# The SSD scan of a hybrid decoder step in three steps per chunk, its elementwise tiles on VectorE, and the scan's mix loaded as whole tiles

## The chip, the cores and the metric

The kernel runs on 1 core of one Trainium2 chip. The metric is the device time of one launch in microseconds; three launches of the kernel before are shown. TensorE is called PE below, its weight loads PEld, VectorE DVE, ScalarE ACT, GpSimd POOL, and SP is the engine from whose queue the transfers here are issued.

## The reference, cut to what matters

One step of a one-layer decoder: a prompt of 1024 tokens and 8 samples of 8 new tokens each (64 rows) go through one input projection, two parallel mixers, one output projection, a squared-ReLU MLP and a final norm, all in float32. The mixers are an HGRN2 recurrence of 8 heads and a Mamba-2 SSD scan of 16 heads in 2 groups of 8. The change is in the second.

```python
log_a = (dt * a)...; xdt = xs * dt[..., None]
cum = jnp.cumsum(log_a, axis=2)                       # per chunk of 128 tokens
seg = cum[:, :, :, None] - cum[:, :, None, :]
decay = jnp.exp(jnp.where(causal, seg, -jnp.inf))
cb = jnp.einsum('cbtgn,cbsgn->cbtsg', cm, bm)
y_intra = jnp.einsum('cbtsg,cbtsgr,cbsgrp->cbtgrp', cb, decay, xdt)
...
def step(s, inp):                                     # over the chunks, in order
    y = jnp.einsum('btgn,bgrpn->btgrp', c_c, s) * fs_c[..., None]
    s = cd_c[..., None, None] * s + jnp.einsum('bsgn,bsgr,bsgrp->bgrpn', b_c, te_c, xdt_c)
    return s, y
...
y = y + d_skip[:, None] * xs
y = rmsnorm(y * silu(z), m_norm)                      # per group of 512 columns
mix = concatenate([o_hg, y]);  x = x + mix @ w_out
```

The samples run the same step with their own state per sequence (`state_ssm`), with 8 tokens as one chunk.

## The kernel before, in words

The kernel goes through its stages in this order: norm and the first chunk of the value projection (`stage01`, with `dt_math`, which leaves `cum`, `te`, `fs` and `cd` in SBUF and the transposed `cum` in DRAM as `cumd`), the SSD stage (`ssd`), the HGRN2 heads (`hgrn`), the output projection (`outproj`), and the MLP (`up_phase`, `down_phase`). Most products are made of three float32r products of high and low parts (`mm3`); the small ones of the scan are plain float32, which the trace shows as two records for each.

The SSD stage in program order: six tiles of the convolution for group 0 (`conv_tile`, whose results go to DRAM as `xtd`, `bcd`, `btd`), the gate columns `z_chunk` 0 and 1 (to DRAM as `szd`), the eight chunks of group 0 in two halves (`ssd_half`), the sample rows of group 0 (`ssd_sample`), `z_chunk` 2 and 3, the six other convolution tiles, the sample rows of group 1, the eight chunks of group 1, and `v_chunk` 1 to 3, the rest of the value projection.

A planner orders the instructions of each engine before launch: it takes the program order as the priority, lets later work through where an earlier instruction is not ready by its assumed durations, and thereby puts matmuls of `z_chunk`, `conv_tile`, `v_chunk` and of the first HGRN2 head between those of the scan. At run time each engine goes through its own list in that order and waits where an operand is late. Transfers are issued from the queue of SP, in order as well.

One chunk of the scan before, by line: three loads (`em` L645, the broadcast rows of `cumd`, 128x1024; `sz` L647; `x` L649); on POOL the subtraction of `cum` from `em` (L650), on DVE the minimum with 0 (L651), on ACT one exponential of 128x1024 (L652), on DVE the product with the masked B-C product `cbm` (L653); in `ssd_x` `xdt` on DVE (L695), `te` on POOL (L696) and the skip term on DVE (L697); the matmuls `pyi` (L658), `pdd` (L660) and eight of `py` (L671); the new state from POOL (L663) and DVE (L666); the output from DVE (L672, L674) and POOL (L676); then `ssd_out`: the gate on POOL (L704), the square on ACT (L706), `rstd` in six small steps on DVE and ACT (L162 to L168), the scale on ACT (L708), four transposes `pyt` (L711) and the product with `m_norm` on DVE (L713), stored to `mixd`.

In `ssd_sample`, for each of four pairs of heads and each half of the eight sequences, the state is transposed and split, two matmuls of 512 columns (L766, L767) apply it to all rows, and `own_sequence` (L244) copies each row's own part out of the four with four predicated copies on DVE.

The last HGRN2 head is followed by `mix_half` (L831): sixteen loads of half tiles (128x544) of the scan's part of the mix, eight for the first half of the tokens (t = 0) and eight for the second, each split into a high part on ACT (L202) and a low part on DVE (L203). The first product of `outproj` needs all eight of t = 0. The raw tiles take slots of the ring `wk` (10 slots of 128x1088), which the head's own work tiles use too; the split parts lie where the normalised input lay, which is read last by the head's gate product.

Of the kernel before, what the change touches and what calls it, by code (L numbers as in the profile page):

```python
# [15 lines left out]
P = 128  # L16
# [3 lines left out]
NB = 8  # L20
# [37 lines left out]
class Kernel:  # L58
# [146 lines left out]
    def mm3(self, ps, sh, sl, mh, ml, start, stop):  # L205
        nc = self.nc
        nc.tensor.matmul(ps, sh, mh, start=start, stop=False)  # L207
        nc.tensor.matmul(ps, sh, ml, start=False, stop=False)  # L208
        return nc.tensor.matmul(ps, sl, mh, start=False, stop=stop)  # L209
# [15 lines left out]
    def per_sequence(self, pool, hi, lo, name, tag=None):  # L225

        gp = self.nc.gpsimd
        oh = pool.tile([P, NB, P], F32R, name=self.nm(name + "h"), tag=tag or name + "h", bufs=4 if tag else 1)
# [115 lines left out]
    def tm_gemm(self, wt, i, tot, pool):  # L344
# [10 lines left out]
        if i == NC:  # L355
            t = pool.tile([P, 260], F32, name=self.nm("st"), tag="st", bufs=3)[0:NS, :tot]
# [5 lines left out]
    def v_chunk(self, pool, j, s0=None, dtb=None, wt=None):  # L362
# [7 lines left out]
        for i in range(NT):  # L370
# [4 lines left out]
            ps = self.tm_gemm(wt, i, 260, pool)  # L375
            rows = P if i < NC else NS
            st = pool.tile([P, 260], F32, name=self.nm("st"), tag="st", bufs=3)
# [6 lines left out]
    def z_chunk(self, pool, j):  # L384
# [3 lines left out]
        for i in range(NT):  # L388
            ps = self.tm_gemm(wt, i, 256, pool)
            rows = P if i < NC else NS  # L390
            R = slice(0, rows)
            st = pool.tile([P, 260], F32, name=self.nm("sz"), tag="st", bufs=3)
# [3 lines left out]
            nc.sync.dma_start(self.szd[i * P:i * P + rows, 256 * j:256 * (j + 1)], st[R, 0:256])  # L396

    def stage01(self):
        nc, a, cst = self.nc, self.a, self.cst
        with self.tc.tile_pool(name="s0", bufs=2) as s0:  # L400
# [20 lines left out]
            self.v_chunk(s0, 0, s0, dtb, wt)  # L421
# [103 lines left out]
    def ssd(self):  # L525
        nc, a = self.nc, self.a
        with ExitStack() as es:
# [3 lines left out]
            self.cs = g.tile([P, 12, 27], F32, name="cs", bufs=1)  # L531
            for f in (10, 8, 0, 1, 2, 3):
                self.conv_tile(f)
            self.z_chunk(g, 0)
            self.z_chunk(g, 1)
            st = self.ssd_half(0, 0, None)
            st = self.ssd_half(0, 1, st)
            self.ssd_sample(0)
            self.z_chunk(g, 2)
            self.z_chunk(g, 3)  # L540
            self.ssd_final(0, st)
# [11 lines left out]
            self.ssd_sample(1)  # L553
            st = self.ssd_half(1, 0, None)
            st = self.ssd_half(1, 1, st)
            self.ssd_final(1, st)
            self.v_chunk(g, 1)
            self.v_chunk(g, 2)
            self.v_chunk(g, 3)

    C2 = {"sz": 3, "x": 3, "xdt": 3, "te": 2, "st": 3, "ms": 2}
# [4 lines left out]
    def em(self, name, shape):  # L566
        return self.g.tile(shape, F32, name=self.nm(name), tag="em", bufs=4)
# [60 lines left out]
    def ssd_half(self, gi, hf, st):  # L628
        nc, a, g, ps = self.nc, self.a, self.g, self.ps
        h0 = gi * 8  # L630
        sl = slice(hf * 512, (hf + 1) * 512)
        bt, ct, btok, cbm = (g.tile([P, 4, P], F32, name=self.nm(t), tag=t, bufs=b)
                             for t, b in (("bt", 1), ("ct", 2), ("btok", 2), ("cbm", 1)))
        nc.sync.dma_start(bt, self.bcd[gi][:, sl].rearrange("p (c t) -> p c t", c=4))
        nc.sync.dma_start(ct, self.bcd[2 + gi][:, sl].rearrange("p (c t) -> p c t", c=4))
        nc.sync.dma_start(btok, self.btd[gi][sl, :].rearrange("(c p) n -> p c n", p=P))
        pc = ps.tile([P, 4, P], F32, name=self.nm("pcb"), tag="sm", bufs=3)
        for j in range(4):
            nc.tensor.matmul(pc[:, j, :], bt[:, j, :], ct[:, j, :], start=True, stop=True)
        nc.vector.tensor_tensor(out=cbm, in0=pc, in1=bc(self.tri, 1, 4), op=ALU.mult)  # L640
        for j in range(4):
            c = 4 * hf + j
            rows = slice(c * P, (c + 1) * P)
            em = self.em("em", [P, 8, P])
            nc.sync.dma_start(em, self.cumd[c * MH + h0:c * MH + h0 + 8, :].partition_broadcast(P))  # L645
            sz = self.c2("sz", [P, 512])
            nc.sync.dma_start(sz, self.szd[rows, gi * 512:(gi + 1) * 512])  # L647
            x = self.c2("x", [P, 8, HD])
            nc.sync.dma_start(x.rearrange("p h d -> p (h d)"), self.xtd[rows, gi * 512:(gi + 1) * 512])  # L649
            nc.gpsimd.tensor_tensor(out=em, in0=em, in1=bc(self.cum[:, c, h0:h0 + 8], 2, P), op=ALU.subtract)  # L650
            nc.vector.tensor_scalar(out=em, in0=em, scalar1=0.0, scalar2=None, op0=ALU.min)  # L651
            nc.scalar.activation(em, em, AF.Exp)  # L652
            nc.vector.tensor_tensor(out=em, in0=em, in1=bc(cbm[:, j, :], 1, 8), op=ALU.mult)  # L653
            xdt, te = self.ssd_x(x, P, c, h0)
            pi = None
            if c > 0:
                pi = ps.tile([P, 512], F32, name=self.nm("pyi"), tag="sm", bufs=3)
                nc.tensor.matmul(pi, ct[:, j, :], st, start=True, stop=True)  # L658
            pd = ps.tile([P, 512], F32, name=self.nm("pdd"), tag="sm", bufs=3)
            nc.tensor.matmul(pd, btok[:, j, :], te.rearrange("p h d -> p (h d)"), start=True, stop=True)  # L660
            stn = self.c2("st", [P, 512])
            if c > 0:
                nc.gpsimd.tensor_tensor(out=stn.rearrange("p (h d) -> p h d", d=HD),  # L663
                                        in0=st.rearrange("p (h d) -> p h d", d=HD),
                                        in1=bc(self.cd[:, c, h0:h0 + 8], 2, HD), op=ALU.mult)
                nc.vector.tensor_tensor(out=stn, in0=pd, in1=stn, op=ALU.add)  # L666
            else:
                nc.vector.tensor_copy(stn, pd)
            py = ps.tile([P, 8, HD], F32, name=self.nm("py"), tag="sm", bufs=3)
            for h in range(8):  # L670
                nc.tensor.matmul(py[:, h, :], em[:, h, :], xdt[:, h, :], start=True, stop=True)  # L671
            nc.vector.tensor_tensor(out=x, in0=py, in1=x, op=ALU.add)  # L672
            if c > 0:
                nc.vector.tensor_tensor(out=xdt, in0=pi.rearrange("p (h d) -> p h d", d=HD),  # L674
                                        in1=bc(self.fs[:, c, h0:h0 + 8], 2, HD), op=ALU.mult)
                nc.gpsimd.tensor_tensor(out=x, in0=x, in1=xdt, op=ALU.add)  # L676
            st = stn
            self.ssd_out(gi, x.rearrange("p h d -> p (h d)"), sz, P, c * P)
        return st
# [887 lines left out]
```

## Time and profile before

| what | value |
|---|---|
| median of 3 runs | 1862.22 us (1861.55 to 1867.1) |
| profiled execution, its own time | 1862.58 us |
| its span, first to last instruction | 1860.9 us |
| PE busy | 1804.0 us, 97% of the span |
| DVE busy | 1346.1 us, 72% |
| ACT busy | 866.9 us, 47% |
| POOL busy | 558.1 us, 30% |
| PE's granted clock, mean | 0.991 of full speed |

The span leaves out 1.7 us of the profiled execution's own time. PE is busy almost throughout, so the places to look at are the few stretches in which it is not, and those in which its clock is below 1.00.

### The profile page before, as it was taken

The page shows a single profiled execution, that of the slowest core. Times are in us where ns is not written, and L with a number is a line of the kernel's source. Part 1 is how long each engine was busy: PE and PEld are TensorE (multiplying, and loading weights), DVE is VectorE, ACT ScalarE, POOL GpSimd, SP SyncE. Part 2 cuts the span into 40 slices and gives each one's busy share as a digit, 9 for nine tenths or more (in the row PEclk, how much of TensorE's full clock was granted, in tenths as well). Part 3 has the DMA queues.
Part 4 walks back from the last instruction along what each step waited for, and adds up shares of the span by engine and source line. Part 5 has one row for each costly group of instructions (what it writes and reads, how often), then busy time and mean ns, then how long its engine had stood idle before and what let it go on. Part 6 is the DMA issues. An engine that isn't in the chain of part 4 may idle for free.

```text
span 1860.9 us, 35593 instructions
## 1 busy us (share of the span) xinstructions
PE 1804.0 (97%) x13352; PEld 1734.6 (93%) x13352; DVE 1346.1 (72%) x2599; ACT 866.9 (47%) x1897; POOL 558.1 (30%) x606
## 2 busy tenths in 40 slices
PE   7999999998999999999899999999999999999998
PEld 7999889997899999999799998999999989999998
DVE  7677888858867766666864477987888767777863
ACT  8575445733254444444532464545554453323322
POOL 5413552226642223323300122222233223222320
PEclk9999999999999999999999999999999999999999
DMA  8444455455442222222276762555555675755621
GB/s 265 123 127 137 133 145 148 121 168 167 124 115 72 63 82 61 82 84 73 78 237 200 226 182 78 190 179 197 199 202 196 208 267 192 267 178 193 210 90 71
DMA packets 329495, 285.47 MB, mean 153 GB/s; under 512 B 26197, under 2 KB 268481, under 8 KB 329322
## 3 DMA queue, kind: packets, MB, share of 16 engines
q1 hardware_dynamic: 329322, 283.19, 48.7%
q8 instruction: 105, 1.72, 0.4%
q14 instruction: 68, 0.56, 0.1%
HBM read 184.61 MB, written 98.24 MB: 152 GB/s over the span
## 4 chain that ended last, share of the span: by engine, by line
PE 77%; DVE 9%; DMA 6%; ACT 3%; issue 2%; POOL 2%; SPq 1%; DVEq 0%; POOLq 0%; ACTq 0%
PE sx L1299 15%; PE mm L209 11%; PE mm L208 11%; PE mm L207 11%; PE sy L1299 7%; PE sz L1299 4%; DVE wl L203 2%; PE mk L207 1%; PE mk L209 1%; PE mk L208 1%; DMA wr<-in_w_down_dram 1%; PE pf L207 1%; PE pf L208 1%; PE pf L209 1%; DMA em<-cumd 1%
## 5 line engine op out<-in xcount | busy, mean ns | idle before, releaser
L202 ACT CAST wh<-wr 128x512 fp32r<-128x512 f32 (+3 forms) x354 | 203.1, 582 | 256.1 <-PE mm L208 98.6
L203 DVE TENSOR_TENSOR wl<-wr,wh 128x512 fp32r<-128x512 f32 (+3 forms) x354 | 237.2, 675 | 93.8 <-ACT wh L202 88.3
L209 PE MATMUL mm<-hh,wl 128*128 128x384 f32 (+1 forms) x840 | 279.7, 333 | 0.0
L207 PE MATMUL mm<-hh,wh 128*128 128x384 f32 (+1 forms) x840 | 277.6, 330 | 1.9 <-ACT raw L584 1.9
L208 PE MATMUL mm<-hl,wh 128*128 128x384 f32 (+1 forms) x840 | 279.0, 332 | 0.0
L1299 PE MATMUL sx<-th,wh 128*128 128x272 f32 x1248 | 243.0, 290 | 5.8 <-ACT u L1350 2.9
L1299 PEld LDWEIGHTS sx<-th,wh 128*128 128x128 f32 x1248 | 195.9, 189 | 10.0 <-ACT u L1350 5.3
L1299 PE MATMUL sx<-th,wl 128*128 128x272 f32 x624 | 179.3, 288 | 0.0
L1256 POOL TENSOR_TENSOR ws<-wr 128x384 f32<-128x384 f32 (+2 forms) x35 | 40.8, 1165 | 427.2 <-DMA wr<-in_w_down_dram 195.2
L209 PEld LDWEIGHTS mm<-hh,wl 128*128 128x128 f32 x840 | 158.1, 188 | 4.6 <-issue 3.7
L207 PEld LDWEIGHTS mm<-hh,wh 128*128 128x128 f32 x840 | 158.4, 189 | 3.5 <-ACT raw L584 2.6
L208 PEld LDWEIGHTS mm<-hl,wh 128*128 128x128 f32 x840 | 158.3, 188 | 1.4 <-issue 0.5
L208 PE MATMUL mm<-wl,hh 128*128 128x260 f32 (+1 forms) x512 | 152.4, 298 | 0.0
L207 PE MATMUL mm<-wh,hh 128*128 128x260 f32 (+1 forms) x512 | 151.6, 297 | 0.6 <-ACT hh L307 0.6
L209 PE MATMUL mm<-wh,hl 128*128 128x260 f32 (+1 forms) x512 | 150.1, 294 | 0.0
L1299 PE MATMUL sy<-th,wh 128*128 128x272 f32 x736 | 142.7, 290 | 2.4 <-ACT wh L202 2.3
L1299 PE MATMUL sx<-td,wh 128*128 128x272 f32 x672 | 131.5, 289 | 1.4 <-ACT acc L1442 1.1
L1299 PEld LDWEIGHTS sy<-th,wh 128*128 128x128 f32 x736 | 116.7, 190 | 3.2 <-ACT wh L202 2.7
L1299 PEld LDWEIGHTS sx<-th,wl 128*128 128x128 f32 x624 | 117.6, 189 | 0.2 <-DVE wl L203 0.2
L207 PE MATMUL mm<-mh,wh 128*128 128x272 f32 x384 | 110.0, 290 | 6.6 <-ACT mh L202 4.7
L208 PE MATMUL mm<-ml,wh 128*128 128x272 f32 x384 | 110.6, 289 | 0.0
L209 PE MATMUL mm<-mh,wl 128*128 128x272 f32 x384 | 110.1, 288 | 0.0
(510 smaller groups left out, 4937.8 us busy)
## 6 DMA issues: line engine op xcount, KB each, us to landing
td<-th SPq DMA_DIRECT2D x112, 272.0 KB, 3.0
td<-td SPq DMA_DIRECT2D x112, 272.0 KB, 5.5
wr<-in_w_in_dram SPq DMA_DIRECT2D x44, 512.0 KB, 4.3
wr<-in_w_out_dram SPq DMA_DIRECT2D x32, 512.0 KB, 4.5
wr<-in_w_up_dram SPq DMA_DIRECT2D x32, 512.0 KB, 4.2
u2d<-u SPq DMA_DIRECT2D x50, 272.0 KB, 2.2
ur<-u2d SPq DMA_DIRECT2D x50, 272.0 KB, 5.1
wr<-in_w_down_dram SPq DMA_DIRECT2D x64, 192.0 KB, 2.9
```

Source lines behind the costliest of these rows:

```text
L202: nc.scalar.copy(hi, x)
L203: (engine or nc.vector).tensor_tensor(out=lo, in0=x, in1=hi.bitcast(F32), op=ALU.subtract)
L207: nc.tensor.matmul(ps, sh, mh, start=start, stop=False)
L208: nc.tensor.matmul(ps, sh, ml, start=False, stop=False)
L209: return nc.tensor.matmul(ps, sl, mh, start=False, stop=stop)
L1256: (engine or self.nc.gpsimd).tensor_tensor(out=out_, in0=x, in1=y, op=op)
L1299: nc.tensor.matmul(acc, w_[:, k, :], b_[:, cols], start=first and k == 0 and q == 0, stop=k == nk - 1 and q == 2, skip_group_check=True)
```

## The change

- The scan of a group is one function, `ssd_group`, in three steps per chunk: `ssd_pre` (loads), `ssd_mid` (`ssd_x` and the decay), `ssd_prod` (the matmuls, state and output sum), and after them `ssd_end` (`ssd_out`). In program order the loads of chunk c+1 come ahead of the products of chunk c, then the decay of chunk c+1, then the end of chunk c-1.
- No large tile of the chunk is worked on by POOL: `te`, the decayed state, the sum of both output parts and the gate product go to DVE. The decay no longer subtracts: DVE takes the minimum of `em` and the broadcast `cum` (tensor-tensor instead of tensor-scalar), and ACT makes eight exponentials of 128x128, one per head, each with the negated `cum` (`ncum`) as its bias.
- The `em` loads of group 0 get an ordering edge behind the last matmul of the first six convolution tiles (`mark`).
- `ssd_sample`: eight masked copies of `cts` are laid into a zeroed tile `cm` on POOL, and sixteen matmuls of 128 columns per pair of heads add up each row's own part in PSUM; the predicated copies are gone, and ACT copies the result out. The sample rows of group 0 come after all eight chunks.
- Buffers: `em` 5 instead of 4, `xdt` 2 instead of 3; the staging tiles of `z_chunk` and `v_chunk` come from the ring `res` (4) instead of `st` (3).
- The scan's mix is loaded as eight whole tiles (128x1088). Four loads, with the splits of t = 0, come in program order ahead of the sample rows of the last head, four behind them; the splits of t = 1 follow from the same tiles.

The diff, cut to its core:

```diff
+            self.mark = self.last_mm
...
+    def ssd_group(self, gi):
+        if gi:
+            self.ssd_sample(gi)
+        self.ssd_pre(gi, 0)
+        self.ssd_mid(gi, 0)
+        for c in range(NC):
+            if c + 1 < NC:
+                self.ssd_pre(gi, c + 1)
+            st = self.ssd_prod(gi, c, st)
+            if c + 1 < NC:
+                self.ssd_mid(gi, c + 1)
+            if c:
+                self.ssd_end(gi, c - 1)
+        self.ssd_final(gi, st)
+        self.ssd_end(gi, NC - 1)
+        if gi == 0:
+            self.ssd_sample(gi)
...
+        ld = nc.sync.dma_start(em, self.cumd[c * MH + h0:c * MH + h0 + 8, :].partition_broadcast(P))
+        if gi == 0:
+            self.after(ld, self.mark)
...
+    def decay(self, em, cbm, rows, c, h0):
+        nc.vector.tensor_tensor(out=em, in0=em, in1=bc(self.cum[0:rows, c, h0:h0 + 8], 2, em.shape[2]), op=ALU.min)
+        for h in range(8):
+            nc.scalar.activation(em[:, h, :], em[:, h, :], AF.Exp, bias=self.ncum[0:rows, c, h0 + h:h0 + h + 1])
+        nc.vector.tensor_tensor(out=em, in0=em, in1=bc(cbm, 1, 8), op=ALU.mult)
...
-                nc.gpsimd.tensor_tensor(out=stn.rearrange("p (h d) -> p h d", d=HD),
+            nc.vector.tensor_tensor(out=stn.rearrange("p (h d) -> p h d", d=HD),
...
-        nc.gpsimd.tensor_tensor(out=te[r], in0=xdt[r], in1=bc(self.te[r, c, h0:h0 + 8], 2, HD), op=ALU.mult)
+        nc.vector.tensor_tensor(out=te[r], in0=xdt[r], in1=bc(self.te[r, c, h0:h0 + 8], 2, HD), op=ALU.mult)
...
-        nc.gpsimd.tensor_tensor(out=y[r_], in0=y[r_], in1=sz[r_], op=ALU.mult)
+        nc.vector.tensor_tensor(out=y[r_], in0=y[r_], in1=sz[r_], op=ALU.mult)
...
+        cm = g.tile([P, NB, 2, NB, TS], F32R, name=self.nm("cm"), tag="em", bufs=5)
+        nc.gpsimd.memset(cm.bitcast(F32), 0.0)
+        for b in range(NB):
+            nc.gpsimd.tensor_copy(cm[:, b, :, b, :], cts.bitcast(F32).rearrange("p (a b t) -> p a b t", a=2, t=TS)[:, :, b, :])
...
-                nc.tensor.matmul(pi, cts, sth, start=True, stop=False)
-                nc.tensor.matmul(pi, cts, stl, start=False, stop=True)
-                self.own_sequence(yf[:, j, :], pi, 4 * hf)
+                for q in range(4):
+                    b = 4 * hf + q
+                    for i, st_ in enumerate((sth, stl)):
+                        nc.tensor.matmul(pi, cm[:, b].rearrange("p a s t -> p (a s t)"), st_[:, q, :],
+                                         start=b == 0 and i == 0, stop=b == NB - 1 and i == 1)
+            nc.scalar.copy(yf[:, j, :], pi)
...
+    def mix_ssd(self, ks):
+        for k in ks:
+            m = self.g.tile([P, T], F32, name=self.nm("mraw"), tag="wk", bufs=10)
+            self.nc.sync.dma_start(m, self.mixd[KO + k])
+            self.mraw.append(m)
+            self.mix[1, 0].append(self.mix_part(m[:, 0:TH]))
+    def mix_other(self):
+        self.mix[1, 1] = [self.mix_part(m[:, TH:]) for m in self.mraw]
...
+        if h == NH - 1:
+            self.hs.close()
...
+            self.mix_ssd(range(4))
```

## Rows read from the trace of the kernel before

**Rows 1.** The page, part 1: busy time, share and instructions of each engine.

```profile
PE 1804.0 (97%) x13352; PEld 1734.6 (93%) x13352; DVE 1346.1 (72%) x2599; ACT 866.9 (47%) x1897; POOL 558.1 (30%) x606
```

**Rows 2.** Windows: PE, PEld, DVE, ACT, POOL busy us (instructions), clock, DMA share, GB/s.

```profile
165.00:262.00 97.00, 91.82 (x685) 83.34 (x684) 83.71 (x147) 43.94 (x113) 55.49 (x34) 0.98 0.49 148
424.00:520.00 96.00, 84.95 (x571) 74.66 (x570) 76.95 (x122) 31.94 (x74) 65.64 (x53) 0.93 0.46 137
440.00:445.00 5.00, 4.32 (x8) 2.26 (x9) 4.93 (x10) 1.46 (x3) 4.30 (x3) 0.50 0.30 104
912.00:947.00 35.00, 26.93 (x222) 24.12 (x221) 30.28 (x57) 19.86 (x39) 8.78 (x5) 0.95 0.54 165
```

**Rows 3.** PE in order of time; in brackets its idle time before, and releaser.

```profile
90.62 0.44 PE L207 MATMUL mm<-hh,wh 128*128 128x384 f32 x1 [1.26 <-ACT raw L584]
213.75 0.66 PE L711 MATMUL pyt<-ident,x 128*128 128x128 f32 x4 [2.12 <-ACT x L708]
440.68 2.07 PE L658 MATMUL pyi<-st,ct 128*128 128x512 f32 x2 [5.09 <-DVE st L668]
471.66 1.12 PE L711 MATMUL pyt<-ident,x 128*128 128x128 f32 x4 [3.27 <-ACT x L708]
924.49 0.87 PE L207 MATMUL mm<-mh,wh 128*128 128x272 f32 x3 [4.72 <-ACT mh L202]
```

**Rows 4.** All engines in order of time, ahead of the wait at 440.68.

```profile
434.15 1.26 POOL L782 TENSOR_TENSOR x<-x,xdt 64x512 f32<-64x512 f32 x1
435.49 1.60 POOL L704 TENSOR_TENSOR x<-x,sz 64x512 f32<-64x512 f32 x1
435.88 4.14 DVE L653 TENSOR_TENSOR em<-em,cbm 128x1024 f32<-128x1024 f32 x1
439.94 0.68 DVE L668 COPY st<-pdd 128x512 f32<-128x512 f32 x1
```

**Rows 5.** DVE's groups from 165 to 262: count, busy us, mean ns of one.

```profile
L174 DVE TENSOR_SCALAR sz<-sz 128x256 f32<-128x256 f32 (+1 forms) x20 | 11.9, 598 | 5.0 <-ACT sz L393 4.8
L653 DVE TENSOR_TENSOR em<-em,cbm 128x1024 f32<-128x1024 f32 x8 | 9.4, 1209 | 0.0
L166 DVE TENSOR_TENSOR yr128t<-yr128t,yr128m 128x1 f32<-128x1 f32 x7 | 5.9, 836 | 0.1
L651 DVE TENSOR_SCALAR em<-em 128x1024 f32<-128x1024 f32 x4 | 3.8, 953 | 0.0
L697 DVE TENSOR_TENSOR x<-x,dsk 128x512 f32<-128x512 f32 x5 | 3.4, 682 | 0.0
L167 DVE TENSOR_SCALAR yr128t<-yr128t 128x1 f32<-128x1 f32 x6 | 0.9, 148 | 0.1
```

**Rows 6.** The same, from 262 to 335.

```profile
L244 DVE COPY_PREDICATED ms<-seqm,pis 128x128 f32<-128x128 uint32 x32 | 9.6, 300 | 1.1 <-PE pis L767 0.5
L174 DVE TENSOR_SCALAR sz<-sz 128x256 f32<-128x256 f32 (+1 forms) x8 | 2.6, 321 | 0.3 <-ACT sz L393 0.3
```

**Rows 7.** ACT's groups from 60 to 560, shapes apart.

```profile
L493 ACT ACTIVATE te<-te 128x128 f32<-128x128 f32 x1 | 0.3, 309 | 0.0
```

**Rows 8.** PE in order of time: the sample rows' products, and one of float32.

```profile
407.92 0.39 PE L766 MATMUL pis<-stb,cts 128*128 128x512 f32 x1
408.15 0.40 PE L767 MATMUL pis<-stb,cts 128*128 128x512 f32 x1
...
424.13 1.05 PE L639 MATMUL pcb<-ct,bt 128*128 128x128 f32 x8
```

**Rows 9.** The chain that ended last, in order of time: two pieces.

```profile
174.96 1.73 PE py L671 x16
...
473.54 5.62 DMA sz<-szd
```

**Rows 10.** SP's queue from 909 to 946: the mix loads.

```profile
919.67 13.94 SPq L831 DMA_DIRECT2D mraw<-mixd  x8
935.05 6.18 SPq L831 DMA_DIRECT2D mraw<-mixd  x8
```

More of the change, by code (lines that the diff above doesn't have):

```diff
@@ L208, in mm3 @@
         nc.tensor.matmul(ps, sh, ml, start=False, stop=False)
-        return nc.tensor.matmul(ps, sl, mh, start=False, stop=stop)
+        self.last_mm = nc.tensor.matmul(ps, sl, mh, start=False, stop=stop)
+        return self.last_mm
     def hilo(self, pool, x, n, name):
@@ L342, in tm_weight, with stage, tm_gemm @@
         return split if later else split()
-    def tm_gemm(self, wt, i, tot, pool):
+    def stage(self):
+        return self.io.tile([P, 384], F32, name=self.nm("st"), tag="res")
+    def tm_gemm(self, wt, i, tot):
         nc = self.nc
@@ L360, in tm_gemm, with v_chunk @@
         return ps
-    def v_chunk(self, pool, j, s0=None, dtb=None, wt=None):
+    def v_chunk(self, j, s0=None, dtb=None, wt=None):
         nc = self.nc
@@ L420, in stage01 @@
             self.gain_columns(lrow)
-            self.v_chunk(s0, 0, s0, dtb, wt)
+            for _ in self.v_chunk(0, s0, dtb, wt):
+                pass
             self.dt_math(s0, nega)
@@ L552, in ssd @@
                 nc.sync.dma_start(a["o_cvs"][0, :, :, cols].rearrange("b j c -> (b j) c"), crow[3:27, :])
[L553 to L561, printed above, removed]
+            self.ssd_group(1)
+            for j in range(1, 4):
+                for _ in self.v_chunk(j):
+                    pass
+    C2 = {"sz": 3, "x": 3, "xdt": 2, "te": 2, "st": 3, "ms": 2}
     def c2(self, name, shape):
@@ new lines, in ssd_prod @@
+    def ssd_prod(self, gi, c, st):
+        nc, ps = self.nc, self.ps
+        h0, j = gi * 8, c % 4
+        em, x, sz, ct, btok, cbm, xdt, te = self.ch[c]
+        pi = None
+        if c > 0:
+            pi = ps.tile([P, 512], F32, name=self.nm("pyi"), tag="sm", bufs=3)
+            nc.tensor.matmul(pi, ct[:, j, :], st, start=True, stop=True)
+        pd = ps.tile([P, 512], F32, name=self.nm("pdd"), tag="sm", bufs=3)
+        nc.tensor.matmul(pd, btok[:, j, :], te.rearrange("p h d -> p (h d)"), start=True, stop=True)
+        stn = self.c2("st", [P, 512])
+        if c > 0:
+            nc.vector.tensor_tensor(out=stn.rearrange("p (h d) -> p h d", d=HD),
+                                    in0=st.rearrange("p (h d) -> p h d", d=HD),
+                                    in1=bc(self.cd[:, c, h0:h0 + 8], 2, HD), op=ALU.mult)
+            nc.vector.tensor_tensor(out=stn, in0=pd, in1=stn, op=ALU.add)
+        else:
+            nc.vector.tensor_copy(stn, pd)
+        py = ps.tile([P, 8, HD], F32, name=self.nm("py"), tag="sm", bufs=3)
+        for h in range(8):
+            nc.tensor.matmul(py[:, h, :], em[:, h, :], xdt[:, h, :], start=True, stop=True)
+        if c > 0:
+            nc.vector.tensor_tensor(out=te, in0=pi.rearrange("p (h d) -> p h d", d=HD),
+                                    in1=bc(self.fs[:, c, h0:h0 + 8], 2, HD), op=ALU.mult)
+        nc.vector.tensor_tensor(out=x, in0=py, in1=x, op=ALU.add)
+        if c > 0:
+            nc.vector.tensor_tensor(out=x, in0=x, in1=te, op=ALU.add)
+        return stn
@@ L823, in slot, with mix_part, mix_half @@
         return getattr(self, pool).tile([P, TH], dtype, name=self.nm(name), tag=tag, bufs=n)
-    def mix_half(self, half, t, raw=None):
+    def mix_ssd(self, ks):
[6 more added lines that the diff above has]
+        self.mix[1, 1] = [self.mix_part(m[:, TH:]) for m in self.mraw]
+    def mix_part(self, m):
+        hi, lo = (self.slot(n, F32R) for n in ("mh", "ml"))
+        self.split(hi, lo, m)
+        return hi, lo
+    def mix_half(self, half, t):
         out = []
         for k in range(KO):
-            hi, lo = (self.slot(n, F32R) for n in ("mh", "ml"))
-            m = raw() if raw else self.slot("mraw", left=True)
+            m = self.slot("mraw", left=True)
             self.nc.sync.dma_start(m, self.mixd[half * KO + k][:, t * TH:(t + 1) * TH])
-            self.split(hi, lo, m)
-            out.append((hi, lo))
+            out.append(self.mix_part(m))
         return out
```

135 lines of the change are left out of this document (59 added, 76 removed).

## The prediction

> **What bounds the kernel now.** I read the page's part 1 first: PE is busy 97% of the span [rows 1], so the kernel is PE's instruction stream, and a change can win only where PE waits, where its clock is low, or by shortening that stream. Next, windows over the stretches that the diff touches [rows 2]. In the scan of group 0 (165 to 262) PE is idle 97.0 - 91.8 = 5.2 us, and its clock of 0.98 loses another 0.02 x 91.8 = 1.8. In the scan of group 1 (424 to 520) it is idle 11.1 us and a clock of 0.93 loses 0.07 x 85.0 = 5.9. At the turn to the output projection (912 to 947) it is idle 8.1 us and 0.05 x 26.9 = 1.3 go to the clock. That is 7.0, 17.0 and 9.4 us: all that the change can win there. Between 262 and 400 there is nothing to win from PE, which is never idle.
>
> Then the order of time on PE, for what ended its waits [rows 3]: transposes that wait for the scaled output (ACT L708), a product that waits for the state (DVE L668), one of the convolution that waits for its staging copy, and the first product of the output projection that waits for its split operand. What lies behind the longest in the scan, 5.09 us, is seen on all engines [rows 4]: the product of 128x1024 on DVE, which takes 1.21 us as a rule [rows 5], lasts 4.14 us here, from 435.88 to 440.02, while POOL works on its own tiles without a break; the state copy stands behind it in DVE's queue. The same hold is seen in the small steps of `rstd`: L166 works on 128x1 and takes 836 ns on average, where L167, of the same size, takes 148 [rows 5]. So POOL's large tiles hold up DVE, DVE's queue then brings operands late, and PE's list, planned without that hold, waits. After the wait of 5.09 us PE also runs on at the lower of its two clock levels: 440 to 445 shows a granted clock of 0.50, that is 1.2 GHz [rows 2].
>
> **What moves to DVE.** Per chunk four products of 128x512 come over from POOL, at 0.68 us each (L697 [rows 5]); the first chunk of a group lacks two. Over eight chunks that is 30 x 0.68 = 20.4 us. The minimum becomes tensor-tensor: I price it like L653 at 1.21, since both read two tiles of 128x1024. In 165 to 262 only four of group 0's minima lie now (3.8 us; the others ran during the convolutions), and after the change all eight, 9.7 us: +5.9. Back come the holds: L166 (836 - 148) x 7 = 4.8; its two siblings in `rstd`, as an estimate, as much together; L174 (598 - 321) x 20 = 5.5, by its mean in 262 to 335 where POOL does little [rows 5, 6]. That is 15.1. Group 0's stretch goes from 83.7 to 83.7 + 26.3 - 15.1 = 95 us of DVE in 97. So DVE becomes as scarce there as PE, and I let only 2 of the 7.0 us come back. Group 1's stretch has 77.0 now; with 20.4 for the products, about 1 for the minima (already held up now) and the holds taken back by the same two-thirds of an estimate, 12, it ends near 86 of 96 while PE's work there is 85.0 - 5.9 = 79. Its fill, `v_chunk` 1 to 3, asks little of DVE, so I let 12 of 17.0 come back; the bounds are 6 (what DVE's spare time alone would allow with its queue as uneven as now) and all 17.0.
>
> ACT makes eight exponentials of 128x128, at 0.31 us each [rows 7] 2.5 us per chunk, 20 us per stretch. Added to 43.9 and 31.9 [rows 2] it stays under 65 of 97, so I cost it at nothing; were ACT full, it would be 1.4 us per chunk.
>
> **The loads.** The `em` loads of group 0 are planned behind the convolutions. The edge sits on loads alone, and the loads behind them in SP's queue (`x`, `sz`) feed the same chunks. It takes POOL's four early subtractions and DVE's four minima out of the convolution stage. I count the wait at 90.62, 1.3 us [rows 3], as gone; bounds 0 and 1.3. The added `em` slot and the fourth staging slot cost nothing while PE is not waiting for either.
>
> **The sample rows.** Removed: 64 predicated copies of 0.30 us, 19.2 us of DVE in two groups (the 32 of one group stand in [rows 6]). They lie where PE is never idle, so they return nothing by themselves. PE's stream grows. Now 32 products of 512 columns run at the spacing 408.15 - 407.92 = 0.23 us, 7.4 us in all [rows 8]. After it there are 128 products of 128 columns. The trace before has no float32r product that narrow. By columns alone one would cost a quarter of 0.23, 0.058: 7.4 us in all, no change. Priced like float32, eight records of 128 columns in 1.05 us, two to a product, 0.26: 33.6 us, +26.2 [rows 8]. Between them stands the row I take: `py`, 64 columns wide, comes at 1.73 / 16 = 0.108 us per record [rows 9], more than its columns need, and each product has a weight load of its own (13352 and 13352 [rows 1]). So 128 x 0.108 = 13.8, and the cost is +6.4 us. All of it lies on PE's path.
>
> The Trainium skill, in "TensorE: Matmul & The Clock Gate", section "Back-to-back issue gap", gives about 81 ns for a load-and-multiply pair of 128 columns; by it the cost would be 128 x 0.081 - 7.4 = 3.0 us, an estimate. No row here has such a product in float32r; the `py` rows are slower than the page's figure, so the sum stays with them.
>
> POOL's zeroing of `cm` and eight small copies come once per group, while PE has convolution and `v_chunk` work as cover; without it they would cost some 3 us a group, by 1.26 us for 512 columns [rows 4].
>
> **The mix.** The first eight half loads leave SP's queue over 13.9 us from 919.67, the next eight over 6.2 us from 935.05 [rows 10]. Now four whole tiles may come earlier, as soon as slots of `wk` and the space of the normalised input are free, and their products can fill the 4.72 us before 924.49 [rows 3]. Against that, t = 0 now needs all eight whole tiles, twice the bytes, and the raw tiles hold eight of ten `wk` slots, so the sample rows of the last head wait for theirs. Bounds: at best 9.4 back; at worst the first product ends when the last bytes come, 941 instead of 935, some 6 us lost. Between ends so far apart I take 3 back.
>
> **The sum.** 12 + 2 + 1.3 + 3 = 18.3 back, 6.4 paid: 11.9 us net. The profiled execution took 1862.6 of its own time, so 1850.7; its time is 0.4 above the median of the runs, so I say 1850.5.
>
> **Rivals.** (a) The narrow products cost what float32 does. Speaks for it: no row shows a narrow float32r product at a better price; against it: by its columns it needs a quarter. 1862.6 - 18.3 + 26.2 = 1870.5. It ends slower, by more than 0.3% from 0.24 us a product on; at 0.20 gain and cost cancel.
>
> (b) DVE becomes the bound of group 0's scan. Today it is 83.7 / 97 = 86% busy there; if its 95 us run at that share, the stretch lasts 110, +13, the stalls of group 1 stay too, and only mix and convolution return 4.3: 1862.6 + 13 + 6.4 - 4.3 = 1877.7. For it: a queue in order is hard to fill better. Against: the gaps of DVE are partly its waits for POOL, and the planner has convolution matmuls to put in. The Trainium skill's "Perfetto Trace Analysis", section "Optimizing Scalar/DVE Operations", would move work off a saturated DVE, though it adds that moving it to GpSimd may not help since both share a read port; this change moves work onto DVE, and [rows 4] show the port's side of it.
>
> (c) The stalls go to loads: 473.54 has `sz` 5.62 us on the chain [rows 9], and `x` and `em` come through the same queue. Then half of group 1 (8) and the convolution come back, nothing of the mix: 1862.6 - 9.3 + 6.4 = 1859.7, no measurable change.
>
> (d) All stalls of the scan and more of the mix go: 17 + 5 + 1.3 + 6 = 29.3 back: 1839.7.
>
> **How the numbers follow.** A run of this kernel can tell about 0.3%, 5.6 us, from no change. Forecast 0.46 (its own range 1839 to 1857), (a) 0.12, (b) 0.16, (c) 0.14, (d) 0.12. Faster: the forecast, (d), and a little of (c): 0.60. Slower: (b) and a part of (a): 0.21. The rest, 0.19, is same. The range, 1838 to 1872, leaves out most of (b) and the lower end of (d).
>
> **What would show it.** Right: POOL almost empty in both scans; L166's mean near 0.15 us; no DVE operation of 128x1024 over 1.3; PE idle in group 1's scan under 5 us with a clock near 1.00; `pis` spaced near 0.11. Wrong: a spacing of 0.2 or more; DVE at 98% for most of group 0's scan with PE waiting on it; waits of PE or DVE that end at `x`, `sz` or `em` loads; or a longer PE wait ahead of the first mix product.

## The result, and the profile after

The changed kernel took 1874.97 us (median of 5 runs, 1872.91 to 1876.9), the kernel before 1862.72 on the same chip (1861.55 to 1867.1): a ratio of 1.0053, 95% interval 1.004 to 1.0067. It is 0.5% slower. The forecast was 1850.5, faster; the time lies above the range of 1838 to 1872.

Below, *lost* means PE's idle time in a stretch plus what its clock takes, (1 - granted clock) x busy, both read from the windows, as in the prediction. Part 1 of the page after, beside [rows 1]:

```profile
PE 1813.3 (97%) x13448; PEld 1746.3 (93%) x13448; DVE 1332.6 (71%) x2599; ACT 894.4 (48%) x2033; POOL 432.3 (23%) x540
```

Windows of the kernel after, with the columns of [rows 2]:

```profile
125.00:150.00 25.00, 19.71 (x148) 19.45 (x146) 18.91 (x33) 22.25 (x65) 1.48 (x8) 0.96 0.73 213
150.00:175.00 25.00, 20.93 (x133) 18.93 (x134) 18.27 (x34) 12.00 (x37) 0.00 (x0) 0.77 0.24 75
225.00:250.00 25.00, 22.56 (x141) 20.60 (x142) 19.21 (x49) 11.42 (x34) 0.20 (x1) 0.80 0.38 116
424.00:520.00 96.00, 95.32 (x706) 86.65 (x705) 82.85 (x154) 46.39 (x139) 7.44 (x16) 1.00 0.58 175
500.00:600.00 100.00, 96.73 (x645) 91.61 (x645) 71.71 (x134) 43.95 (x84) 22.20 (x42) 0.98 0.33 91
900.00:975.00 75.00, 68.19 (x472) 62.09 (x472) 58.13 (x127) 32.27 (x69) 11.49 (x7) 0.93 0.49 150
```

Group 1's scan has healed: 424 to 520 loses 0.7 us, where it lost 17.0. Group 0's has not. From 125 to 175 PE loses (5.29 + 0.04 x 19.71) + (4.07 + 0.23 x 20.93) = 15.0 us, where the kernel before lost nothing, and 225 to 250 another 7.0. Behind the scans 500 to 600 loses 5.2, and the turn to the output projection (900 to 975) 6.8 + 0.07 x 68.19 = 11.6.

PE in order of time shows the waits, as in [rows 3]:

```profile
154.07 2.08 PE L706 MATMUL pdd<-te,btok 128*128 128x512 f32 x2 [9.36 <-DVE te L745]
448.28 1.89 PE L717 MATMUL py<-xdt,em 128*128 128x64 f32 x15 [0.68 <-DVE em L690]
551.30 1.12 PE L1010 MATMUL pke<-ident,ke 128*128 128x128 f32 x4 [2.76 <-DVE ke L975]
941.08 1.12 PE L1171 MATMUL pot<-ident,hsq 128*128 128x128 f32 x4 [3.74 <-DVE hsq L1168]
```

One wait of 9.36 us stands ahead of the first product of the scan. The chain that ended last shows what lies before it:

```profile
131.48 4.82 DMA em<-cumd
...
136.32 1.24 DVE em L687
...
138.40 2.06 ACT em L689 x7
140.46 0.36 ACT tok L628
...
140.85 5.24 DMA xtd<-tok
...
146.11 2.58 DMA x<-xtd
...
148.72 0.69 DVE xdt L744
...
149.41 3.41 DVE em L690 x3
...
153.42 0.61 DVE te L745
...
154.07 2.08 PE pdd L706 x2
```

Read it backwards: `te` stands in DVE's queue behind three products of 128x1024, those behind `xdt`, `xdt` behind the load of `x`, that load behind the store of the convolution's result (`xtd`), and the store behind the copy `tok` on ACT, ahead of which seven of the small exponentials took 2.06 us. All decay work of five chunks is squeezed in here, behind the edge. ACT's groups from 131 to 155, with count, busy us and mean ns:

```profile
L689 ACT ACTIVATE em<-em,ncum 128x128 f32<-128x128 f32 x40 | 12.6, 399 | 1.3 <-DVE em L687 1.3
```

ACT is busy for 22.25 of 25 us from 125 to 150. Its busy share alone does not make the stall: the kernel before had it busy for 21.84 us there, and PE waited for nothing.

### The profile page after: what moved, and what is told of

Its sections match the earlier page's. It is cut to its first block, busy times and chain, and to the rows that moved or that the text cites. A ratio compares the mean times of both kernels' runs of the same rounds, so it can differ in the third digit from the quotient of the medians.

```text
span 1873.3 us, 35753 instructions
## 1 busy us (share of the span) xinstructions
PE 1813.3 (97%) x13448; PEld 1746.3 (93%) x13448; DVE 1332.6 (71%) x2599; ACT 894.4 (48%) x2033; POOL 432.3 (23%) x540
## 4 chain that ended last, share of the span: by engine, by line
PE 79%; DMA 8%; DVE 8%; ACT 3%; issue 2%; POOL 0%; SPq 0%; DVEq 0%; ACTq 0%; POOLq 0%
PE sx L1372 15%; PE mm L209 12%; PE mm L208 11%; PE mm L207 11%; PE sy L1372 7%; PE sz L1372 4%; PE py L717 1%; DVE wl L203 1%; PE mk L209 1%; PE mk L207 1%; PE mk L208 1%; DMA em<-cumd 1%; DMA wr<-in_w_down_dram 1%; PE pf L207 1%; PE pf L208 1%
## 5 line engine op out<-in xcount | busy, mean ns | idle before, releaser
L203 DVE TENSOR_TENSOR wl<-wr,wh 128x512 fp32r<-128x512 f32 (+3 forms) x354 | 232.0, 661 | 93.1 <-ACT wh L202 87.0
L1372 PEld LDWEIGHTS sx<-th,wh 128*128 128x128 f32 x1248 | 195.9, 189 | 12.3 <-ACT u L1423 5.5
L208 PE MATMUL mm<-wl,hh 128*128 128x260 f32 (+1 forms) x512 | 147.8, 289 | 0.0
```

Source lines behind the costliest of these rows:

```text
L203: (engine or nc.vector).tensor_tensor(out=lo, in0=x, in1=hi.bitcast(F32), op=ALU.subtract)
L1372: nc.tensor.matmul(acc, w_[:, k, :], b_[:, cols], start=first and k == 0 and q == 0, stop=k == nk - 1 and q == 2, skip_group_check=True)
```

## The experiments

Each run was compared with launches of the kernel before on the same chip; the ratio is to those, with its 95% interval. Different runs come from different chips, so where two runs are compared with each other the ratios are safer than the medians. Each trace is of one execution.

**The edge, taken out and put in alone.** The first run drops two lines from the changed kernel, the second adds the edge alone to the kernel before.

```
-        if gi == 0:
-            self.after(ld, self.mark)
```

> The changed kernel without the ordering edge on group 0's em loads. Theory A (the edge makes the loss): the em loads go out near 71 us again, the decay is done before the first products, the wait of 9.4 us ahead of the first pdd (144.7 to 154.1) and its low clock go, and the time falls by 10 to 15 us, to about 1860 to 1865; the wait of 1.3 us in the convolutions may come back. Rival B (the new program order puts the first pdd too early whatever the loads do, since x is stored and loaded back only at 146): the wait stays at 5 us or more, and the time falls by less than 5 us.

> The kernel before with nothing but the ordering edge on group 0's em loads. Theory A in its plain form (late em loads are harmful by themselves): 5 to 10 us slower than before, with a wait ahead of the first pdd near 167. Rival C (the edge harms only a scan whose first products are planned at 145; before they stand at 167): no change within 0.3%, with the wait of 1.3 us in the convolutions gone.

Without the edge: 1872.81 us, 1.0035 (1.0022 to 1.0048). The edge alone on the kernel before: 1882.6, 1.0085 (1.0071 to 1.01). So the edge alone harms, by more than the 5 to 10 us expected, but taking it out of the changed kernel gives little. The wait only moves: without the edge PE is busy for 49.95 of the 50 us from 125 to 175, but 75 to 100 now loses 9.7. Rival B's time came, but not its reason, since no long wait is left at the first `pdd`. PE in order of time without the edge:

```profile
96.75 0.69 PE L207 MATMUL mm<-hh,wh 128*128 128x384 f32 x1 [6.84 <-ACT raw L591]
```

The loads now land in the middle of the convolutions, and the copy `raw`, which frees PE's output, comes late on ACT: the chain before it runs through the exponentials of five chunks, and then through convolution steps on DVE that they had made late.

**The reading of the sample rows, and the mix, each as before.** Changed kernel with 32 products of 512 columns and predicated copies; changed kernel with the half-tile loads.

```
-                        nc.tensor.matmul(pi, cm[:, b]..., st_[:, q, :], ...)   # 128 columns
+                nc.tensor.matmul(pi, cts, sth, start=True, stop=False)         # 512 columns
+                nc.tensor.matmul(pi, cts, stl, start=False, stop=True)
+                self.own_sequence(yf[:, j, :], pi, 4 * hf)
```

> The changed kernel with the sample rows' state read as before (products of 512 columns and predicated copies on DVE). Theory: 128 products at 0.104 us against 32 at 0.23 cost PE 5.9 us, so the time falls by about 6 us, to 1869. Rival: the predicated copies, 19.2 us of DVE, are felt now that DVE has more to do, and the time stays or rises.

> The changed kernel with the scan's mix loaded as sixteen half tiles behind the last head, as before. Theory: whole tiles brought no gain, since the raw tiles take the slots that the sample rows need and the first product waits for twice the bytes; idle and clock losses from 900 to 975 fell by nothing, so the time falls by 1 to 3 us. Rival: whole tiles gained the 3 us of the forecast, hidden by shifts elsewhere, and the time rises by about 3 us.

Old reading: 1875.11 us, 1.0048 (1.0034 to 1.0062). Old mix: 1875.49, 1.0052 (1.0032 to 1.0071). Neither is measurably different from the whole change. For the reading that is what its rival had, but that the predicated copies on DVE are the reason is not shown. With the old reading PE has less to do, but 125 to 175 loses 17 us in place of 15, 500 to 600 loses 9 in place of 5, and its wait at the start of the scan was longer:

```profile
154.76 2.08 PE L706 MATMUL pdd<-te,btok 128*128 128x512 f32 x2 [10.36 <-DVE te L745]
```

**How the decay is made, with and without the edge.** The minimum and eight exponentials become subtraction, minimum and one exponential, in both groups: the subtraction on DVE with the edge, on POOL with it, and on POOL without.

```
-        nc.vector.tensor_tensor(out=em, in0=em, in1=bc(self.cum...), op=ALU.min)
-        for h in range(8):
-            nc.scalar.activation(em[:, h, :], em[:, h, :], AF.Exp, bias=self.ncum...)
+        nc.vector.tensor_tensor(out=em, in0=em, in1=bc(self.cum...), op=ALU.subtract)   # or nc.gpsimd
+        nc.vector.tensor_scalar(out=em, in0=em, scalar1=0.0, scalar2=None, op0=ALU.min)
+        nc.scalar.activation(em, em, AF.Exp)
```

> The changed kernel with the edge, but the decay of a chunk made by a subtraction and a minimum on DVE and one exponential of 128x1024 on ACT, in place of the tensor-tensor minimum and eight exponentials of 128x128. Theory A (ACT): the 40 exponentials of 0.31 us for five em tiles (12 us) that stand in ACT's queue between 131 and 155 delay the convolution's and z_chunk's work and the decays themselves; one of 128x1024 takes 1.06 us, so some 7 us leave ACT's burst, and DVE gets about 0.7 us more per chunk. The wait of 9.36 us at 154 falls to 5 or less, group 0's loss from 23 to 17 or less, the time to 1866 to 1870. Rival B (loads): the wait ends when em and x arrive, so it stays near 9 and the time near 1875. Rival C (DVE): DVE's queue holds te behind the em products, and gets longer; the wait grows to 10 or more and the time to 1876 to 1880.

> The changed kernel with the edge, but the decay as before: subtraction on POOL, minimum on DVE, one exponential of 128x1024. Theory A (ACT): like the run with the subtraction on DVE, 1866 to 1870, and POOL takes the wait for em out of DVE's queue, which gives 1 to 3 more; against it the large POOL tiles hold up DVE again, so some of group 1's 16 us come back as stalls (up to 5). Rival B (loads): wait at 154 near 9, 1875. Rival R (the three-step order makes group 0's loss whatever makes the decay): 1873 to 1877.

> The changed kernel without the edge and with the decay as before (POOL subtraction, DVE minimum, one exponential). POOL, which is idle in the convolutions, waits for em there, and ACT has 5 x 1.06 instead of 40 x 0.31 us. Theory A with first touch: the waits of 6.84 us at 97 (without the edge) and of 9.36 at 154 (with it) are both absent, 50 to 175 loses 5 to 8 us as in the kernel before (5.3), and the time is 1858 to 1866 with the part of group 1's stalls that the large POOL subtractions bring back. Rival R (the three-step order makes the loss): 50 to 250 loses over 18 us and the time is 1871 to 1877. Rival B (loads): as with the edge removed, 1872.

DVE, edge: 1875.16 us, 1.0056 (1.0042 to 1.007). POOL, edge: 1883.62, 1.0101 (1.0086 to 1.0117). POOL, no edge: 1869.2, 1.0032 (1.002 to 1.0044). The second is above every range that was expected, the third lies between its two. By the total, one exponential behind the edge gave nothing, against theory A. In group 0 it gave most of what theory A said: the wait of 9.36 us is gone, and 125 to 275 loses 10.2 + 0.06 x 139.8 = 18.6 us where the change loses 24.0. The longest waits of the first run are now:

```profile
150.56 0.39 PE L207 MATMUL mm<-wh,hh 128*128 128x256 f32 x1 [4.17 <-DVE st L400]
532.02 1.11 PE L760 MATMUL pyt<-ident,x 128*128 128x128 f32 x4 [4.27 <-ACT x L757]
```

This run changes group 1's decay as well, and there 500 to 600 loses 7.9 where the change loses 5.2; 50 to 125 loses 2 more too. So its total does not tell what one exponential is worth behind the edge.

Between the second and the third the edge alone makes 14 us. Most of what the third still loses against the change lies in group 1, where POOL's large subtraction is back: 424 to 520 loses 11.3 us there, where the change loses 0.7. DVE and PE in order of time:

```profile
430.32 2.55 DVE L203 TENSOR_TENSOR wl<-wr,wh 128x520 fp32r<-128x520 f32 x1
...
434.66 3.67 PE L715 MATMUL py<-xdt,em 128*128 128x64 f32 x16 [6.00 <-DVE em L688]
```

The step on DVE takes 0.68 us elsewhere; here POOL subtracts from 430.43 to 432.32. Two more of DVE's steps in this chain, at 422.80 and 426.33, take 2.39 us beside POOL's subtractions.

**The square in group 0: first engine against number of exponentials.** No edge; group 1 as in the change; only the decay of group 0 differs. The fourth corner is the run without the edge above.

```
     def decay(self, em, cbm, rows, c, h0):
+        if h0 == 0:
+            return self.decay0(em, cbm, rows, c, h0)
```

> The changed kernel without the edge, with the decay of group 0 alone as before (POOL subtraction, one exponential) and that of group 1 as in the change (no large tile on POOL). Theory A with first touch: group 0 loses about what it lost before (5.3 in 50 to 100, 7.0 in the scan) and group 1 keeps its gain of 16 us, less 5.9 for the narrow products and some 3 for head 0 and the mix: 1862.6 - 16 + 5.9 + 3 = 1855, 1852 to 1860: faster than the kernel before. Rival R (the three-step order): 1871 to 1877.

> No edge; group 1 as in the change; the decay of group 0 begins on DVE (subtraction and minimum) and has one exponential of 128x1024. Beside it stand two runs that differ in group 0's decay alone: minimum on DVE and eight exponentials 1872.8 (1.0035), subtraction on POOL and one exponential 1863.7 (1.0000). Theory T (first touch: the engine that meets the late em loads must not be the busy DVE): about 1870 to 1873, with a wait over 4 us in 50 to 100 that ends at DVE. Theory A (ACT's 40 small exponentials of 12 us between 76 and 92): about 1863 to 1866, and 50 to 100 loses 5 to 7 us as in the kernel before. Half of each: 1867 to 1869.

> No edge; group 1 as in the change; the decay of group 0 begins on POOL (subtraction), has its minimum on DVE and eight exponentials of 128x128 on ACT. Theory T (first touch): about 1862 to 1866. Theory A (ACT): about 1870 to 1873, with the long wait of the convolution at some 97 us behind ACT's exponentials. Half of each: 1867 to 1869.

| group 0's decay begins on | one exponential | eight |
|---|---|---|
| POOL | 1863.66, 1.0000 (0.9989 to 1.0012) | 1879.87, 1.0086 (1.0067 to 1.0104) |
| DVE | 1866.74, 1.0007 (0.9998 to 1.0017) | 1872.81, 1.0035 (1.0022 to 1.0048) |

The columns differ, the rows do not in one direction: theory T falls, and the eight exponentials cost, 6 us on one line and 16 on the other (5 and 16 by the ratios). Both runs with POOL came out slower than theory A had said (1852 to 1860 with one, 1870 to 1873 with eight). With one exponential and no edge the time is that of the kernel before, or near it, though the narrow products are still there: taking away both burdens gave back 9 to 10 us by the ratios, where taking away the edge alone gave 3.

The same is seen in the stage itself. Windows from 50 to 275: first the kernel before, then four kernels whose decay of group 0 begins on DVE, with neither burden, with the edge (the run above with one exponential in both groups), with the eight exponentials, and with both (the change):

```profile
50.00:275.00 225.00, 217.45 (x1559) 206.49 (x1558) 172.32 (x339) 127.35 (x324) 87.55 (x94) 0.98 0.46 135
50.00:275.00 225.00, 218.51 (x1539) 208.34 (x1538) 174.02 (x373) 127.66 (x318) 27.53 (x58) 0.96 0.45 134
50.00:275.00 225.00, 213.69 (x1475) 204.16 (x1475) 161.71 (x347) 124.42 (x306) 19.62 (x57) 0.95 0.41 123
50.00:275.00 225.00, 210.45 (x1475) 200.08 (x1474) 165.24 (x357) 134.99 (x374) 21.90 (x59) 0.95 0.44 127
50.00:275.00 225.00, 210.86 (x1464) 200.26 (x1464) 163.27 (x352) 134.74 (x365) 22.31 (x56) 0.94 0.43 127
```

They lose 11.9, 15.2, 22.0, 25.1 and 26.8 us. Each burden alone costs 7 to 10 us, both together 11.6: with one of them there, the other adds 2 to 5. Rival R, the three-step order itself, is left with the 3 us between the first two.

ACT's groups from 74 to 97, first with eight (begun on DVE), then with one (begun on POOL):

```profile
L687 ACT ACTIVATE em<-em,ncum 128x128 f32<-128x128 f32 x40 | 12.6, 392 | 3.7 <-issue 3.7
```

```profile
L696 ACT ACTIVATE em<-em 128x1024 f32<-128x1024 f32 x5 | 5.3, 1058 | 3.4 <-DVE em L695 3.4
```

And the chain that ended last of the run with eight exponentials begun on POOL, up to the convolution's product that waited 4.64 us:

```profile
89.44 1.05 ACT em L697 x6
...
90.85 0.60 ACT acc L602
...
92.16 1.41 ACT em L697 x7
93.56 0.38 ACT ce L608
93.94 0.37 ACT raw L591
...
94.36 0.69 PE mm L207
```

The exponentials of chunks that are needed 60 us later run ahead of the copy that PE needs at once. In this run they are cheaper one by one than in the change (seven in 1.41 us), yet the loss is larger; a second wait of 4.59 us at 128.34 ends a chain of DVE work, not of exponentials. So the size is not ACT's time alone; the planner makes a new order for each program, and what that does was not tested by itself. Only the direction is settled.

**The reading again, on the mended kernel.** No edge, group 0's decay from POOL with one exponential, group 1 as in the change, and the sample rows read as before.

> The run with no edge, group 0's decay from POOL and group 1 as in the change (1863.7), and with the sample rows read as in the kernel before (32 products of 512 columns and predicated copies). If the narrow products' 128 x 0.104 - 7.4 = 5.9 us lie on the path: 1857.8 (1855 to 1860). Rival (the predicated copies on DVE fill DVE's queue, as in the earlier run with the old read): 1862 to 1866.

1856.31 us, 0.9957 (0.9943 to 0.997): faster than both kernels, and 7 us (by the ratios 8) below the same kernel with narrow products. PE's busy time fell from 1807.4 to 1802.9. The saving that was invisible in the changed kernel, where the stalls grew as it came, now shows.

**The edge on the fastest kernel.** Only the two lines of the edge are added.

> The fastest run so far (1856.3) with the edge alone added: group 0's em loads wait for the last product of the convolutions. If the edge harms whatever stands behind it (9 to 17 us in the three pairs so far with one exponential): 1865 to 1872, with a PE wait over 4 us in 145 to 175. Rival (it harmed only beside other burdens): 1854 to 1858.

1880.23 us, 1.0085 (1.0066 to 1.0104): 24 us for two lines, more than the range expected. The same windows, first of the fastest kernel, then with the edge:

```profile
125.00:150.00 25.00, 25.00 (x184) 24.91 (x184) 19.75 (x44) 22.05 (x55) 3.92 (x11) 1.00 0.35 102
150.00:175.00 25.00, 25.00 (x199) 23.57 (x199) 21.32 (x39) 10.29 (x27) 1.43 (x1) 1.00 0.49 156
```

```profile
125.00:150.00 25.00, 20.19 (x150) 19.93 (x149) 22.27 (x30) 15.78 (x35) 13.28 (x13) 0.97 0.70 197
150.00:175.00 25.00, 19.85 (x148) 19.11 (x149) 17.02 (x33) 12.85 (x30) 0.00 (x0) 0.89 0.24 77
```

The DMA share in the first window doubles, and POOL's work there goes from 3.92 to 13.28 us. DVE, POOL and PE in order of time, with the edge:

```profile
139.56 4.87 DVE L605 SCALAR_TENSOR_TENSOR acc<-raw,prm,acc 128x384 f32<-128x384 f32 x3
144.36 2.38 DVE L697 TENSOR_SCALAR em<-em 128x1024 f32<-128x1024 f32 x1
146.66 1.98 DVE L174 TENSOR_SCALAR st<-st 128x256 f32<-128x256 f32 x1
...
139.67 4.39 POOL L696 TENSOR_TENSOR em<-em,cum 128x1024 f32<-128x1024 f32 x2
144.06 4.43 POOL L696 TENSOR_TENSOR em<-em,cum 128x1024 f32<-128x1024 f32 x2
...
151.92 0.58 PE L207 MATMUL mm<-wh,hh 128*128 128x256 f32 x1 [6.72 <-DVE st L400]
```

All five subtractions fall into 12 us, from 136.55 to 148.49, in which DVE still finishes the convolutions. DVE's steps are held meanwhile (a step of 128x256 that takes 0.29 us in the changed kernel takes 1.98), `z_chunk`'s gate is late, and PE stands. ACT, with one exponential, is busy for only 15.78 us there, so this stall needs no full ACT. These two windows account for 12.7 of the 27.3 us between the two traces (1883.0 and 1855.7); 500 to 550, at the end of group 1's scan, loses another 10.4, and why an edge on group 0 does that is open.

**Group 1's part alone.** Group 0's scan in the old order on the old engines, reading and mix as before, no edge; the second run also has the old buffers of the scan. Both keep the new staging ring of `z_chunk` and `v_chunk`.

```
-    C2 = {"sz": 3, "x": 3, "xdt": 2, ...       # and five "em" slots
+    C2 = {"sz": 3, "x": 3, "xdt": 3, ...       # and four
```

> Group 0's scan wholly in the order and on the engines of the kernel before, sample rows and mix as before; only group 1's scan in three steps without large tiles on POOL. If group 1's gain of 15 to 16 us is a thing of its own and the loss lies in group 0's part and in the reading: 1863.7 - 15 + up to 5 that head 0 and the MLP's spread take back = 1849 to 1855, faster than the kernel before by 0.5 to 0.8%. Rival (what group 1 gains comes back as stalls of the following heads): 1858 to 1863.

> Like the run with group 0 wholly as before and only group 1's scan in three steps (1869.3), but with the buffers of the kernel before: three for xdt in place of two, four for em in place of five. Theory B (buffers): group 0 in its old order needs its third xdt slot; without it 50 to 100 and 200 to 275 lost 8.6 and 13.4 us, with it they fall back to about 4 and 7 and the time to 1850 to 1856. Rival (the planner's orders differ as a whole because the program around differs, and no one edit makes it): group 0 keeps 10 or more and the time stays at 1864 to 1870.

1869.3 us, 1.002 (1.0007 to 1.0033); with the old buffers 1867.09, 1.0013 (1.0001 to 1.0024). Both expectations of a gain fell. Windows of the second run:

```profile
200.00:275.00 75.00, 67.40 (x478) 60.02 (x477) 65.25 (x116) 31.23 (x83) 45.12 (x30) 0.93 0.47 137
424.00:500.00 76.00, 75.85 (x552) 69.17 (x552) 65.22 (x127) 37.80 (x118) 2.80 (x1) 1.00 0.62 187
```

Group 1 loses 0.2 us up to 500, but 500 to 550, its end and the first head, loses 12.0 where the kernel before lost nothing; and group 0 loses 12.3 from 200 to 275 where the kernel before, in nearly the same code, lost 6.6. The first is given back later, as the rival had it. The second stays open: the scan's buffers did not explain it, the staging ring was not tested, and that a program changed elsewhere is ordered differently throughout, the rival whose range the second run met, is argued and not shown.

**One exponential in group 1 too.** The fastest kernel with subtraction, minimum and one exponential on DVE and ACT in group 1.

> The fastest run so far (no edge, group 0's decay from POOL, old read: 1856.3) with group 1's decay made by subtraction and minimum on DVE and one exponential of 128x1024. Theory A says that small exponentials cost where ACT is nearly full; in group 1's scan ACT works 46 of 96 us, so taking them away there gives nothing: 1854 to 1858. Rival (they delay the chain of every chunk by 2.45 - 1.06 = 1.4 us wherever they stand): 1845 to 1851. If DVE, at 83 of 96 there, can't take another 0.65 us a chunk: 1860 to 1864.

1869.54 us, 1.0024 (1.0015 to 1.0034): 13 us slower than the fastest, more than any theory had. The end of group 1's scan, first in the fastest kernel, then in this one:

```profile
500.00:525.00 25.00, 20.95 (x116) 19.12 (x115) 14.55 (x33) 10.00 (x22) 5.42 (x15) 0.86 0.50 141
```

```profile
500.00:525.00 25.00, 16.94 (x76) 12.22 (x76) 20.12 (x45) 6.96 (x20) 2.79 (x14) 0.74 0.31 92
```

DVE works 20.12 us there in place of 14.55, with PE waiting for it. In group 1, where ACT has room and DVE has not, the eight exponentials are the better form. This stretch and the next 25 us account for 5 of the 13; where the rest lies was not found.

## Why the prediction was wrong, point by point

**The step that failed** is the pair that was costed at nothing: the edge ("after the convolutions" was taken as a gain of 1.3 us with no other price; that gain came, 50 to 100 lost 3.8 us before and 2.6 after) and ACT's eight exponentials ("it stays under 65 of 97, so I cost it at nothing"). The second was read from the wrong window. The scan's 97 us do have room (ACT works 51.95 of 97 there after, less than forecast), but with five `em` slots the work of five chunks runs before the scan, as soon as the loads land: 40 exponentials, 12.6 us, in the convolutions (76 to 92) or behind the edge (131 to 155). There ACT had little room already (17.69 of 25 us from 75 to 100 and 21.84 from 125 to 150 in the kernel before). The prediction's own bound, 1.4 us per chunk, would have been 7 us for five chunks; without the edge the runs show 6 and 16. The edge costs 9 to 24 us by the ratios (medians of four pairs in the old code or with one exponential: 1865.6 to 1882.6, 1866.7 to 1875.2, 1869.2 to 1883.6, 1856.3 to 1880.2; in the second pair group 1's decay differs too). The two burdens add only in part: from 50 to 275 either alone costs most of what both do, so taking one away gave little. That these two make the loss in group 0 is shown; how each of them comes to its size is not, since an edge or an exponential also changes the order of everything planned around it.

**Group 0's scan, 2 of 7.0 to come back:** wrong in sign. From 125 to 275 it lost 24 us where it had lost 7. Rival (b) had the direction, and with 1877.7 nearly the time, but not the mechanism: DVE did not become the bound by its sum, it was late at one place, behind loads that the edge held back. The sum itself failed too: 95 of 97 us were forecast for DVE from 165 to 262, with all eight minima inside, and 69.71 were measured. Five of the eight minima ran before 150, three from 150 to 262 (L687 below); that is 6 us of the difference, and the rest was not traced.

**Group 1's scan, 12 of 17.0:** right in mechanism, short in size: 16.3 came back in the stretch, and with POOL's subtraction put back it lost 11.3 again. POOL's holds are gone, as forecast; DVE's groups from 150 to 262, beside [rows 5]:

```profile
L745 DVE TENSOR_TENSOR te<-xdt,te 128x512 f32<-128x512 f32 x8 | 5.5, 684 | 0.0
L687 DVE TENSOR_TENSOR em<-em,cum 128x1024 f32<-128x1024 f32 x3 | 3.7, 1221 | 3.5 <-DMA em<-cumd 3.5
L166 DVE TENSOR_TENSOR yr128t<-yr128t,yr128m 128x1 f32<-128x1 f32 x6 | 0.9, 153 | 0.1
```

The price of a product, 0.68, and of a minimum, 1.21, held; L166 fell from 836 ns to 153. But the prediction stopped at the end of the stretch: right behind it, 500 to 600 now loses 5.2 us, so that 11 of the 16.3 are left; with group 1's part alone and the old buffers it was 12.

**The sample rows, +6.4:** right. PE in order of time:

```profile
287.09 0.89 PE L819 MATMUL pis<-stb,cm 128*128 128x128 f32 x7
287.82 0.62 PE L811 MATMUL pst<-ident,ss 128*128 128x128 f32 x4
```

Seven products in 0.73 us, 0.104 each against 0.108: 128 x 0.104 - 7.4 = 5.9 us. Rival (a) fell. That the price came so near is partly luck, as the row it was taken from is of float32 and half as wide. The first product of each eight stands alone among products of 256 columns and takes only 0.06 us (286.39 to 286.45), what its columns ask, so 5.9 is an upper estimate; the seven in a row cost more. The Trainium skill's 81 ns for such a pair ("TensorE: Matmul & The Clock Gate", section "Back-to-back issue gap") is not reached here; the measurement decides. On the mended kernel the old reading gave 7 us, so "they return nothing by themselves" held: the copies came back with it and cost nothing that can be seen.

**The mix, 3 back:** nothing. 900 to 975 lost 8.1 + 0.02 x 66.9 = 9.4 us before and 11.6 after, and the old mix in the changed kernel made no difference that can be measured.

**The sum, as measured:** 16.3 back in group 1 and 1.2 in the convolutions; paid 17 in group 0 (24 against 7), 5.9 for the products, 5 behind the scan, 2 at the mix: 12.4 net, beside 12.25 by the medians and 12.4 by the two spans (1873.3 - 1860.9). The agreement is luck: the stretches left out here (262 to 400, and all behind 975) lose some 6 us more than before by the same reading, so the reading is good to some 6 us and no better.

## What to carry to other kernels

Price moved work in the stage in which it will run, which its loads and free buffers decide, not in the loop in which it stands in the code: with five buffers, the work of five iterations can run a stage early. An edge that holds loads back also gathers everything behind them, so look at how full each in-order queue is at the moment of release. And where one edit moved back gives nothing, move back pairs: two burdens on one stage can each be enough to stall it, and a saving elsewhere (here the 7 us of the reading) showed only when both were gone. Read the stage beside the total: a run that changes two places can gain in one what it loses in the other.

## What the runs showed of the hardware

One exponential of 128x1024 takes 1.06 us on ACT; eight of 128x128 with a bias column follow one another at 0.31 us (7 in 2.16 in the changed kernel at 138.3), without one at 0.21 (8 in 1.71). Both forms stand in one trace, of the run with eight exponentials begun on POOL: 297 ns on average without the bias column in group 0, 390 with it in group 1. They differ in the bias operand alone as far as the program shows.

After the 9.36 us of waiting PE did not return to full speed at once: of its two levels, 1.2 and 2.4 GHz, it had the lower from 154 to 158 (a granted clock of 0.50) and for most of 158 to 162 (0.56), and full speed from 162. By those windows that made 0.50 x 3.93 + 0.44 x 4.00 = 3.7 us on top of the idle time. The loss read from 150 to 175 as one window, 0.23 x 20.93 = 4.8, is too large, because its mean clock takes in idle time too. The fastest kernel, which does not wait there, shows 1.00 in it.
